# A hybrid decoder step on one core: a second bank for the third products, the last pair's second products one projection later, and the norms of x in two parts

## The chip, the cores and the metric

The kernel runs on one core of one Trainium2 chip. The metric is the device time of one execution in microseconds (us). A core has five engines with a queue each: TensorE (PE; its weight loads are shown apart, as PEld), VectorE (DVE), ScalarE (ACT), GpSimd (POOL) and SyncE (SP, which here only issues DMAs). Each engine works its queue in the order in which it was written, and engines wait for each other by semaphores. TensorE writes its results to PSUM, which has eight banks of 128 x 512 float32; all other tiles lie in SBUF, 128 partitions of one address space.

## The reference

One step of a one-layer decoder for 512 prompt tokens and 8 sequences of 8 new tokens (64 sample tokens) with 2048 cached tokens each. What matters here is the way into the layer and one of its three attention forms, the one over compressed blocks of the cache:

```python
def pre_mixer(x, c, lp):
    mod = jnp.einsum('bd,de->be', jax.nn.silu(c), lp['w_ada']) + lp['b_ada']
    sh1, sc1, gt1, sh2, sc2, gt2 = jnp.split(mod[:, None, :], 6, axis=-1)
    h = rms_norm(x, lp['norm1_g']) * (1.0 + sc1) + sh1
    z = jnp.einsum('btd,dc->btc', h, lp['w_in'])
    ...

def compress_blocks(x, pos, w1, w2):
    ...
    lead = jnp.einsum('bncgd,cdh->bngh', xc + pos[0], w1[0])
    trail = jnp.einsum('bncgd,cdh->bngh', xc + pos[1], w1[1])
    return jnp.einsum('bngh,hd->bngd', jax.nn.silu(lead[:, :-1] + trail[:, 1:]), w2)
```

`compress_blocks` is computed for the raw keys and the raw values (kv = 0 and 1 below) of all cached pages of the 8 sequences; the keys are then RMS-normed. Everything else (attention, the output projection, an MLP) comes later in the kernel and is not touched.

## The kernel before, in words

**The first stage** (`first_stage`, from L549) does two things at once. It compresses the cache of the 8 sequences, and it brings x into its normed, turned and modulated form `hf`.

The cache work is cut into 48 units. Sequences go in four pairs; the sequences of the first two pairs are taken one by one (units 0 to 31, eight for each sequence), those of the last two pairs two at a time (units 32 to 39 and 40 to 47). A unit is one of four quarters j of the taps, for keys or values. The DVE first copies a quarter of the pages into another order (`cmp_order`, tile `ro`, for keys and values together). PE transposes it (`rows_turn`, PSUM tiles `ct`), ACT copies the result to the tile `x`, and DVE or POOL adds its two halves to `xs`. Then come the products of the unit (`cmp_hidden`, L487): the first and second products `hid`, from `x`, into two PSUM banks per pair (one for keys, one for values), and the third products `hids`, from the sums `xs` and the summed weights `w1sum`, into one bank per pair that holds keys and values side by side. When the last quarter of a pair is done, `cmp_act` (L503) reads the banks `hid` (ACT, then DVE), `cmp_silu` (L522) subtracts from the bank `hids` (DVE writes `csx`), and takes the silu (tanh on ACT, a product on DVE, tile `cst`). Some units later `cmp_out` (L532) multiplies that with the second weights (`co`, the second products; ACT squares and a chain of small DVE operations norm the keys, `rms_cols`, L426), and `cmp_keys` (L542) turns the normed keys (`kct`).

The work on x is put in between by a table written by hand, `todo[u]`: lists of functions that run behind unit u. For each of the five tiles of x (four of 128 prompt tokens, one of 64 sample tokens) there is a load on the POOL queue (`load_x`, three buffers), `norm(k)` (`norm_scaled`, L742: ACT squares with a sum, a chain of 12 small DVE operations for the inverse root, `rsqrt`, L139, then ACT multiplies x by the root in place) and three units later `turned(k)` (eight PE transposes `nt` into two PSUM tiles, which ACT copies to `hf`). Eight chunks of the modulation weights are handled likewise: `ada_first` sums a chunk (PE into a PSUM tile `ada`, copied by ACT), and one unit later `ada_end` turns it (PE into a PSUM tile `adat`, read by a DVE reduction `adas`).

PSUM in the first stage (`banks`, L66, called at L2572 with 3): two banks `tr` for `ct`, three banks `mm` that serve `nt`, `ada`, `adat`, `co`, `kct` and a few more, two banks `acc` for `hid`, one bank `cc` for `hids`.

**The order of the work.** While `self.chain` is a string, `link` (L93) ties every PE instruction behind the one before it, so in the first stage and in the first projection PE does exactly the order of the program. The other engines' queues are ordered by the framework's scheduler, by a simulated time; `issue_after` holds an instruction behind another one of the same engine.

**The seam and the projections.** At unit 46 `seam` (L2547) frees the first stage's pool `pe`, splits the eight rows of `hf` into high and low parts (`split_pack`, L825, whose operation on DVE has L829, tiles `h2`) and splits the first two chunks of `w_in` (`winh` on ACT, `winl` on DVE). Behind unit 47 comes the silu of the last pair (`cmp_act` and `cmp_silu` for i = 3, whose tiles lie inside the tile `w1raw`, the first weights, and so appear under that name). Then eight projections follow, `step(0)` to `step(7)` (`project`, L883): each multiplies the five tiles of h with one chunk of 256 or 264 columns of `w_in`, 24 matrix products per prompt tile, 16 for the sample tile. `between` is a list of functions that run behind the products of tile 0, 1, ... In `step(0)` they are: nothing, `cmp_out` for the keys of the last pair, `cmp_out` for its values, `cmp_keys` and `room` (which takes the memory of `w1raw` for the next stage).

**Memory.** SBUF tiles lie in pools that are stacked from the left (`const`, `keep`, `small`, `op`, `pl`, `pe`, and later `op2`, `zn`, `pkq`, `pk`, `pm`, `pq`, `pu`, `pf`, ...) and from the right (`zf`, `pw`, `pc`, `ph`, ...). Every tile takes a multiple of 32 bytes per partition. In `keep` there are two tiles of two float32 each, `cmpb` and `cmpb2`. In the built program the pools on the left behind `keep` (`small`, `op` and those above) start at 32 modulo 64 bytes; the pools on the right start at 0 modulo 64.

Of the kernel before, what the change touches and what calls it, by code (L numbers as in the profile page):

```python
# [6 lines left out]
F32 = mybir.dt.float32  # L7
F32R = mybir.dt.float32r
BF16 = mybir.dt.bfloat16
I32 = mybir.dt.int32  # L10
AF = mybir.ActivationFunctionType
OP = mybir.AluOpType
AX = mybir.AxisListType

P = 128
D = 1024
# [3 lines left out]
NS = 64  # L20
# [3 lines left out]
TOK = 2080  # L24
# [10 lines left out]
TILES = [(0, 128), (128, 128), (256, 128), (384, 128), (512, 64)]  # L35
# [11 lines left out]
class Step:  # L47
# [347 lines left out]
    def cmp_bias(self, pe, kv):  # L395

        if kv == 0:
            self.cmpb = self.keep.tile([P, 2], F32, name="cmpb")
            self.posp = pe.tile([P, 256], F32, tag="posp", bufs=1, name="posp")
        pb = self.mmb(f"posb{kv}")  # L400
        for j in range(4):
            for i in range(4):
                n = 16 * kv + 4 * j + i
                self.mm(pb[32 * i:32 * i + 32, 0:P], self.posT[:, n:n + 1].to_broadcast([P, 32]),
                        self.w1raw[:, kv, 4 * j + i, :], j == 0, j == 3)
        (self.act if kv else self.cp)(self.posp[:, P * kv:P * kv + P], pb[:, 0:P])

    def cmp_bias_end(self):
        tb = self.sideb("posbt")
        for kv in range(2):  # L410
            self.tr(tb[:, P * kv:P * kv + P], self.posp[:, P * kv:P * kv + P])
        self.nc.vector.tensor_reduce(self.cmpb, tb[:, 0:256].rearrange("p (k i r) -> p k r i", k=2, i=4)[:, :, 0, :],
                                     axis=AX.X, op=OP.add)
        self.cmpb2 = self.keep.tile([P, 2], F32, name="cmpb2")
        self.ts(self.cmpb2, self.cmpb, 2.0, None, OP.mult)

    def silu2(self, pool, hb, W, bias, tag, uid, room=None):

# [68 lines left out]
    def cmp_hidden(self, u):  # L487
        i, bs, j, kv = self.units[u]
        first = bs[0] % 2 == 0 and j == 0
        if first and kv == 0:  # L490
            self.hid[i] = [self.accb(f"hid{i}{e}") for e in range(2)] + [self.bank("cc", 1, f"hids{i}")]
        ab, c = self.hid[i][kv], self.hid[i][2]
        x, xs = self.ring[u % 2]
        q, n = P * (bs[0] % 2), P * len(bs)
        for e in range(2):
            for a in range(2):
                self.mm(ab[:, 256 * e + q:256 * e + q + n], self.w1raw[:, kv, 8 - 8 * e + 4 * a + j], x[:, 2 * e + a, q:q + n],
                        first and e + a == 0, j == 3 and a == 1)
        for a in range(2):
            self.mm(c[:, 256 * kv + q:256 * kv + q + n], self.w1sum[:, kv, j, a], xs[:, a, q:q + n],  # L500
                    first and kv + a == 0, j == 3 and a == 1)

    def cmp_act(self, pl, i, kv):  # L503
        if kv == 0:
            self.ths, self.xbs = [], []

        v = self.r1.rearrange("p (n c) -> p n c", c=512)
        xb, th = (v[:, 1 if kv else 8], v[:, 0 if kv else 9]) if i == 3 else (
            pl.tile([P, 512], F32, tag="csx", bufs=2, name=f"csx{i}{kv}"), pl.tile([P, 512], F32, tag="cst", bufs=2, name=f"cst{i}{kv}"))
        ab = self.hid[i][kv]  # L510
        t, y = th[:, 0:256], th[:, 256:512]
        self.act(y, ab[:, 256:512], AF.Identity, bias=self.cmpb[:, kv:kv + 1])
        o = xb.rearrange("p (s c m e) -> p s m e c", s=8, c=8, e=2)
        av, yv = [a.rearrange("p (s m c) -> p s m c", s=8, m=4) for a in (ab[:, 0:256], y)]
        self.tt(o[:, :, 0:3, 1], yv[:, :, 0:3], av[:, :, 1:4], OP.add)
        self.tt(o[:, :, 3, 1, 0:7], yv[:, :, 3, 0:7], av[:, :, 0, 1:8], OP.add)
        self.tt(o[:, :, 3, 1, 7], yv[:, :, 3, 7], ab[:, 32:288].rearrange("p (s c) -> p s c", c=32)[:, :, 0], OP.add)
        self.stt(t, y, self.cmpb2[:, kv:kv + 1], ab[:, 0:256], OP.subtract, OP.add)
        self.ths.append(th)
        self.xbs.append(xb)  # L520
# [11 lines left out]
    def cmp_out(self, pl, i, kv):  # L532
        ob = self.mmb(f"co{i}{kv}")
        for s in range(4):
            self.mm(ob[:, 64 * s:64 * s + 64], self.ths[kv][:, P * s:P * s + P], self.w2[kv], True, True)
        if kv == 0:
            r = self.r1[:, 1024:1536].rearrange("p (n g d) -> p n g d", n=2, d=64) if i == 3 else None
            self.kn = self.rms_cols(pl, ob, P, 4, "kn", f"{i}", None if r is None else (r[:, 0], r[:, 1]))
        else:
            self.cp(self.vc[:, 2 * i:2 * i + 2, :], ob[:, 0:256].rearrange("p (b e) -> p b e", b=2))  # L540
# [8 lines left out]
    def first_stage(self, pl, pe, hf, seam):  # L549
# [3 lines left out]
        self.chain = ""  # L553
        self.sideb = self.mmb
        self.cpg, self.ros, self.hid, self.adas = {}, {}, {}, {}
        xs = []

        def load_x():
            k = len(xs)
# [2 lines left out]

        def norm(k):
            with self.tc.issue_after(self.last_high):
                self.norm_scaled(xs[k], 0, k, xs[k], pl.tile([P, D], BF16, tag="sq", name=f"sq{k}"))

        def turned(k):
            t0, m = TILES[k]
            for h in range(2):
                self.act(hf[:, 4 * h:4 * h + 4, t0:t0 + m], self.norm_turned(xs[k], 0, k, h))  # L570
# [37 lines left out]
        todo = {u: [] for u in range(48)}  # L608
# [3 lines left out]
        todo[10] += [self.ada_turned, lambda: self.cmp_bias(pe, 0), lambda: self.cmp_bias(pe, 1)]  # L612
        todo[12] += [self.cmp_bias_end]

        for k, u in enumerate((23, 25, 27, 29, 33)):
            todo[u - 3] += [lambda k=k: norm(k)]
            todo[u] += [lambda k=k: turned(k)]
        pages = lambda b: lambda: (self.cmp_tile(pe, b), self.cmp_pages("sync", b))
        wada = lambda k: lambda: self.ada_first_load(pe, ada[k])
# [119 lines left out]
        for a in range(3):  # L739
            self.tt(self.Dt[:, :, 4 * a, :], xv, pv[:, :, a + 1], OP.add)  # L740

    def norm_scaled(self, sq, n, i, x, junk=None):  # L742

        t0, m = TILES[i]
        ss = self.small.tile([P, 1], F32, tag="nss", name=f"nss{n}_{i}")
        self.squares = self.act((sq if junk is None else junk)[:m], x[:m], AF.Square, accum_out=ss[:m]).ins
        rs = self.small.tile([P, 1], F32, tag="nrs", name=f"nrs{n}_{i}")
        self.rsqrt(rs[:m], ss[:m], 1.0 / D)
        if n:
            self.ts(sq[:m], x[:m], rs[:m], None, OP.mult)  # L750
        else:
            self.act(sq[:m], x[:m], scale=rs[:m])

    def norm_turned(self, sq, n, i, h):

# [1769 lines left out]
    def run(self):  # L2525
        nc, I, O, keep = self.nc, self.I, self.O, self.keep
# [16 lines left out]
        lctx, actx, zctx, pctx = [ExitStack() for _ in range(4)]  # L2543
        pl, pe = self.pool("pl", lctx), self.pool("pe", actx)
        h2 = []

        def seam():  # L2547

            actx.close()
            self.zfp = self.pool("zf", zctx, side="right")  # L2550
            self.zF = self.zfp.tile([P, 4, C_N], F32, tag="zF", bufs=1, name="zF")
            self.pw, self.pc, ph = [self.pool(n, pctx, side="right") for n in ("pw", "pc", "ph")]
            last = self.splits[-1], self.last_high

            def rows(pins, ks):
                with ExitStack() as c:
                    for i in pins:
                        c.enter_context(self.tc.issue_after(i))
                    for k in ks:
                        h2.append(ph.tile([P, 2 * NT], F32R, name=f"h2_{k}"))  # L2560
                        self.split_pack(h2[k], hf[:, k])
                        self.splits.append(self.packed)

            self.wraw = {}
            self.win_load(self.pw, 0)
            rows(self.behind46, range(3))
            for i in range(2):
                self.win_split(self.pw, 0, i, last)
                rows(last, ((3, 4), (5, 6, 7))[i])

        with ExitStack() as c:
            self.banks("psc", c, 3)  # L2572
            self.first_stage(pl, pe, hf, seam)
        self.banks("ps", self.top, 4)
        lctx.close()
# [6 lines left out]

        self.znp = self.pool("zn", octx)
        self.zN = self.znp.tile([P, 4, TOK - C_N], F32, tag="zN", name="zN")

        def room():
            self.r1 = keep.tile([P, 5 * D], F32, tag="r1", bufs=1, name="r1w")
            self.zS = self.r1[:NS, 0:TOK]

        self.pkq = self.pool("pkq", octx)  # L2590
        kctx = ExitStack()
        pk = self.pool("pk", kctx)
        with pctx:
            pw, pc = self.pw, self.pc
            self.adn, self.ada_open, self.ada_next, self.ada_made = 8, None, None, None

            def step(ci, **kw):
                self.dma("sync", self.hfd[:, ci], h2[ci].bitcast(F32))
                self.project(pw, ci, h2, **kw)
                self.ada_later()  # L2600
                self.stage()

            step(0, between=[lambda: None] + [lambda kv=kv: self.cmp_out(None, 3, kv) for kv in range(2)] + [lambda: (self.cmp_keys(3), room())])
            self.chain = None
            self.cmp_prompt_a(pk, pc)
            self.cmp_prompt_load(pk, 0)
            step(1)
            self.cmp_prompt_b(0)
            self.cmp_prompt_load(pk, 1)
            self.head_norm("sk", C_SK, 2, 1)  # L2610
# [53 lines left out]
        ph = self.pool("p3", self.top, side="right")  # L2664
# [60 lines left out]
```

## Time and profile before

| | |
|---|---|
| Median of 3 runs | 1165.17 us (1164.33 to 1167.17) |
| The profiled execution's own time | 1162.46 us |
| Its span, first to last instruction | 1160.8 us, mean granted clock of TensorE 0.998 |
| First stage, about | 0 to 163 us |
| First projection, about | 163 to 185 us |
| Busy of 30 us, PE / DVE / ACT, from 90 us | 27.80 / 18.10 / 15.50 us |
| the same, from 120 us | 30.00 / 15.51 / 13.15 us |
| the same, from 150 us | 27.02 / 21.26 / 16.94 us |

How to read what follows: a row of the list of waits names the waiting engine, its instruction and what it waited for, then the total in us, how many times, and the longest. A row of the timeline has the start in us from the beginning of the span, the length, the engine, the line of the kernel, the operation, the tile written <- the tiles read, the shapes, the count of instructions merged, and in brackets the idle time ahead of it with what ended it. The end of a matrix product is modelled, so rows of PE overlap a little; the starts are measured. A row of the chain of work that ended last has start, length and what ran. In a table by windows a row has the window, its length, then for PE, PEld, DVE, ACT and POOL the busy time in it and the number of instructions, then the granted clock of TensorE, the mean share of the DMA engines and the GB/s.

### The profile page before, as it was taken

The page shows a single profiled execution, that of the slowest core. Times are in us where ns is not written, and L with a number is a line of the kernel's source. Part 1 is how long each engine was busy: PE and PEld are TensorE (multiplying, and loading weights), DVE is VectorE, ACT ScalarE, POOL GpSimd, SP SyncE. Part 2 cuts the span into 40 slices and gives each one's busy share as a digit, 9 for nine tenths or more (in the row PEclk, how much of TensorE's full clock was granted, in tenths as well). Part 3 has the DMA queues.
Part 4 walks back from the last instruction along what each step waited for, and adds up shares of the span by engine and source line. Part 5 has one row for each costly group of instructions (what it writes and reads, how often), then busy time and mean ns, then how long its engine had stood idle before and what let it go on. Part 6 is the DMA issues. An engine that isn't in the chain of part 4 may idle for free.

```text
span 1160.8 us, 25274 instructions
## 1 busy us (share of the span) xinstructions
PE 1128.4 (97%) x9530; PEld 970.0 (84%) x9530; DVE 763.8 (66%) x1852; ACT 578.4 (50%) x1101; POOL 301.7 (26%) x353
## 2 busy tenths in 40 slices
PE   8889989999999999999999999999999999999998
PEld 6887889999766566777899999789999997888887
DVE  3556474687786895666653545667766754897686
ACT  2365463354776785555532324356565654565420
POOL 4314320000220120001677662001655511101000
PEclk9999999999999999999999999999999999999999
DMA  9997444796684679899889986356454637877732
GB/s 236 248 269 231 127 141 166 240 336 215 196 274 147 207 225 306 292 318 322 228 255 299 335 267 218 101 153 214 133 155 148 193 115 251 318 260 245 223 116 82
DMA packets 188187, 255.51 MB, mean 220 GB/s; under 512 B 23161, under 2 KB 144706, under 8 KB 185890
## 3 DMA queue, kind: packets, MB, share of 16 engines
q1 hardware_dynamic: 148770, 173.03, 48.4%
q0 software_dynamic: 21296, 67.38, 18.0%
q10 hardware_dynamic: 18000, 13.50, 3.9%
q8 instruction: 75, 1.23, 0.4%
q14 instruction: 46, 0.38, 0.1%
HBM read 217.64 MB, written 57.12 MB: 237 GB/s over the span
## 4 chain that ended last, share of the span: by engine, by line
PE 81%; DVE 8%; DMA 6%; SPq 3%; issue 2%; ACT 1%; DVEq 0%; ACTq 0%
PE dn L83 14%; PE z L83 9%; PE mg L83 9%; DMA cpg<-in_cache_nsa_kv 5%; PE br L83 4%; PE wo L83 4%; PE up L83 3%; PE k L89 3%; SPq L168 2%; PE so L83 2%; PE hid L83 2%; PE ss L83 2%; PE dns L83 2%; PE ada L83 2%; PE ct L89 1%
## 5 line engine op out<-in xcount | busy, mean ns | idle before, releaser
L83 PE MATMUL z<-winh,h 128*128 128x264 f32 (+1 forms) x576 | 111.8, 288 | 0.1
L83 PEld LDWEIGHTS z<-winh,h 128*128 128x128 f32 x576 | 92.6, 192 | 1.6 <-issue 0.6
L83 PE MATMUL z<-winl,h 128*128 128x264 f32 (+1 forms) x320 | 88.6, 285 | 0.0
L83 PE MATMUL mg<-hH,wmh 128*128 128x288 f32 x240 | 70.2, 294 | 0.0
L83 PE MATMUL mg<-hH,wml 128*128 128x288 f32 x240 | 70.1, 294 | 0.0
L83 PE MATMUL mg<-hL,wmh 128*128 128x288 f32 x240 | 68.0, 293 | 0.0
L83 PE MATMUL hid<-x,w1raw 128*128 128x128 f32 (+1 forms) x384 | 64.4, 311 | 2.1 <-ACT x L118 2.1
L83 PEld LDWEIGHTS z<-winl,h 128*128 128x128 f32 x320 | 61.2, 191 | 0.1
L83 PEld LDWEIGHTS hid<-x,w1raw 128*128 128x128 f32 x384 | 54.2, 191 | 5.2 <-ACT x L118 2.6
L118 ACT ACTIVATE x<-ct 128x512 f32<-128x512 f32 x64 | 36.4, 594 | 41.9 <-PE ct L89 25.6
L137 DVE TENSOR_TENSOR wml<-wmr,wmh 128x1024 fp32r<-128x1024 f32 x14 | 19.7, 1405 | 43.2 <-ACT wmh L118 43.2
L83 PEld LDWEIGHTS mg<-hH,wmh 128*128 128x128 f32 x240 | 45.1, 188 | 0.1
L83 PEld LDWEIGHTS mg<-hH,wml 128*128 128x128 f32 x240 | 45.0, 187 | 0.0
L83 PEld LDWEIGHTS mg<-hL,wmh 128*128 128x128 f32 x240 | 44.3, 188 | 0.0
L137 DVE TENSOR_TENSOR wp<-sums,wp 128x1024 fp32r<-128x1024 f32 x26 | 36.6, 1415 | 9.7 <-ACT wp L118 9.2
L137 DVE TENSOR_TENSOR wp<-pu,wp 128x512 fp32r<-128x512 f32 (+1 forms) x26 | 30.4, 1176 | 19.1 <-ACT wp L118 15.6
L2083 POOL TENSOR_TENSOR td<-td 128x512 f32<-128x512 f32 x24 | 35.5, 1482 | 18.8 <-DMA td<-in_w_down 18.7
L83 PE MATMUL hids<-xs,w1sum 128*128 128x128 f32 (+1 forms) x192 | 36.1, 310 | 4.2 <-DVE csx L106 4.2
L118 ACT ACTIVATE u<-u 128x1152 f32<-128x1152 f32 x29 | 33.6, 1160 | 11.0 <-DVE u L106 10.3
L2083 POOL TENSOR_TENSOR td<-td,td 128x512 f32<-128x512 f32 x24 | 34.2, 1426 | 16.7 <-DMA td<-in_w_down 16.0
L89 PE MATMUL ct<-identF,ro 128*128 128x128 f32 x256 | 36.1, 275 | 2.3 <-DVE ro L121 2.3
L83 PE MATMUL br<-oH,wbl 128*128 128x288 f32 x128 | 37.8, 295 | 0.0
(1175 smaller groups left out, 3561.8 us busy)
## 6 DMA issues: line engine op xcount, KB each, us to landing
adw<-in_w_ada SPq DMA_DIRECT2D x16, 1024.0 KB
foxD<-in_cache_fox_kv SPq DMA_DIRECT2D x128, 128.0 KB
rows<-in_cache_nsa_kv SPq DMA_DIRECT2D x128, 128.0 KB
rows<-foxD SPq DMA_DIRECT2D x26, 512.0 KB
pu<-in_w_up SPq DMA_DIRECT2D x26, 512.0 KB
wdr<-in_w_down SPq DMA_DIRECT2D x26, 512.0 KB
cpg<-in_cache_nsa_kv SPq DMA_DIRECT2D x96, 128.0 KB
td<-in_w_down POOLq DMA_DIRECT2D x24, 512.0 KB, 6.4
```

Of the source, the lines that this page charges most:

```text
L83: ins = self.nc.tensor.matmul(out, a, b, start=start, stop=stop, skip_group_check=True)
L89: ins = self.nc.tensor.transpose(out, in_, self.identF[:n, :n])
L118: return self.nc.scalar.activation(out, in_, f, **kw)
L137: self.splits.append((eng or self.nc.vector).tensor_tensor(l, x, h.bitcast(F32), op=OP.subtract).ins)
L168: self.issued[eng] = getattr(self.nc, eng).dma_start(out, in_).ins
L2083: self.nc.gpsimd.tensor_tensor(out, x, y, op=OP.subtract)
```

## The change

- `hids` gets two banks (`cc` 1 to 2), taken in turn by the pairs; the shared banks `mm` of the first stage go from three to two, so that it stays at eight.
- `norm(k)` is cut in two: the squares and the inverse root (`norm_root`), and the multiplication of x by it on ACT (`scaled(k)`). They run behind units (18, 20, 22, 28, 29) and (21, 23, 25, 30, 31); before, both ran behind units (20, 22, 24, 26, 30). `turned(k)` stays at 23, 25, 27 and 33, except for the fourth tile, which goes from 29 to 32.
- The second products of the last pair (`cmp_out(3, .)`) and `cmp_keys(3)` move from the first projection into the second: behind its tiles 0, 1 and 3.
- The tile `last_ths` (4 KB per partition, in a pool `pt` of its own on the right) takes the silu of the last pair and the norm of its keys; they no longer lie inside `w1raw`. The tile `r1w` is taken ahead of the first projection.
- `cmpb2` becomes the second half of `cmpb`, so `keep` is 32 bytes shorter, and `small`, `op` and all pools above them on the left move down by 32 bytes, from 32 to 0 modulo 64. The pools on the right stay.

```diff
-            self.cmpb = self.keep.tile([P, 2], F32, name="cmpb")
+            self.cmpb = self.keep.tile([P, 4], F32, name="cmpb")
...
-        self.cmpb2 = self.keep.tile([P, 2], F32, name="cmpb2")
+        self.cmpb2 = self.cmpb[:, 2:4]
...
-            self.hid[i] = [self.accb(f"hid{i}{e}") for e in range(2)] + [self.bank("cc", 1, f"hids{i}")]
+            self.hid[i] = [self.accb(f"hid{i}{e}") for e in range(2)] + [self.bank("cc", 2, f"hids{i}")]
...
-        xb, th = (v[:, 1 if kv else 8], v[:, 0 if kv else 9]) if i == 3 else (
+        xb, th = (v[:, 8 + kv], self.last_ths[:, kv]) if i == 3 else (
...
-            r = self.r1[:, 1024:1536].rearrange("p (n g d) -> p n g d", n=2, d=64) if i == 3 else None
+            r = self.last_ths[:, 0].rearrange("p (n g d) -> p n g d", n=2, d=64) if i == 3 else None
...
         def norm(k):
             with self.tc.issue_after(self.last_high):
-                self.norm_scaled(xs[k], 0, k, xs[k], pl.tile([P, D], BF16, tag="sq", name=f"sq{k}"))
+                roots[k] = self.norm_root(xs[k], 0, k, xs[k], pl.tile([P, D], BF16, tag="sq", name=f"sq{k}"))
+
+        def scaled(k):
+            m = TILES[k][1]
+            self.act(xs[k][:m], xs[k][:m], scale=roots[k])
...
-        for k, u in enumerate((23, 25, 27, 29, 33)):
-            todo[u - 3] += [lambda k=k: norm(k)]
+        for k, (n, v, u) in enumerate(((18, 21, 23), (20, 23, 25), (22, 25, 27), (28, 30, 32), (29, 31, 33))):
+            todo[n] += [lambda k=k: norm(k)]
+            todo[v] += [lambda k=k: scaled(k)]
             todo[u] += [lambda k=k: turned(k)]
...
-            self.pw, self.pc, ph = [self.pool(n, pctx, side="right") for n in ("pw", "pc", "ph")]
+            self.pw, self.pc, ph, pt = [self.pool(n, pctx, side="right") for n in ("pw", "pc", "ph", "pt")]
+            self.last_ths = pt.tile([P, 2, 512], F32, name="cst3")
...
-            self.banks("psc", c, 3)
+            self.banks("psc", c, 2)
...
-            step(0, between=[lambda: None] + [lambda kv=kv: self.cmp_out(None, 3, kv) for kv in range(2)] + [lambda: (self.cmp_keys(3), room())])
+            step(0)
...
-            step(1)
+            step(1, between=[lambda kv=kv: self.cmp_out(None, 3, kv) for kv in range(2)] + [lambda: None, lambda: self.cmp_keys(3)])
```

More of the change, by code (lines that the diff above doesn't have):

```diff
@@ L411, in cmp_bias_end @@
             self.tr(tb[:, P * kv:P * kv + P], self.posp[:, P * kv:P * kv + P])
-        self.nc.vector.tensor_reduce(self.cmpb, tb[:, 0:256].rearrange("p (k i r) -> p k r i", k=2, i=4)[:, :, 0, :],
+        self.nc.vector.tensor_reduce(self.cmpb[:, 0:2], tb[:, 0:256].rearrange("p (k i r) -> p k r i", k=2, i=4)[:, :, 0, :],
                                      axis=AX.X, op=OP.add)
-        self.cmpb2 = self.keep.tile([P, 2], F32, name="cmpb2")
-        self.ts(self.cmpb2, self.cmpb, 2.0, None, OP.mult)
+        self.cmpb2 = self.cmpb[:, 2:4]
+        self.ts(self.cmpb2, self.cmpb[:, 0:2], 2.0, None, OP.mult)
     def silu2(self, pool, hb, W, bias, tag, uid, room=None):
@@ L555, in first_stage @@
         self.cpg, self.ros, self.hid, self.adas = {}, {}, {}, {}
-        xs = []
+        xs, roots = [], {}
         def load_x():
@@ L740, in forget_sums, with norm_root @@
             self.tt(self.Dt[:, :, 4 * a, :], xv, pv[:, :, a + 1], OP.add)
-    def norm_scaled(self, sq, n, i, x, junk=None):
+    def norm_root(self, sq, n, i, x, junk=None):
         t0, m = TILES[i]
@@ L748, in norm_scaled @@
         self.rsqrt(rs[:m], ss[:m], 1.0 / D)
[L749 to L752, printed above, removed]
+        return rs[:m]
+    def norm_scaled(self, sq, n, i, x, junk=None):
+        m = TILES[i][1]
+        self.ts(sq[:m], x[:m], self.norm_root(sq, n, i, x, junk), None, OP.mult)
     def norm_turned(self, sq, n, i, h):
@@ L2584, in run @@
         self.zN = self.znp.tile([P, 4, TOK - C_N], F32, tag="zN", name="zN")
-        def room():
-            self.r1 = keep.tile([P, 5 * D], F32, tag="r1", bufs=1, name="r1w")
-            self.zS = self.r1[:NS, 0:TOK]
+        self.r1 = keep.tile([P, 5 * D], F32, tag="r1", bufs=1, name="r1w")
+        self.zS = self.r1[:NS, 0:TOK]
         self.pkq = self.pool("pkq", octx)
```

## The prediction

> **What bounds the kernel now.** I read the page first: busy time, then the chain that ended last by engine.
>
> ```profile
> span 1160.8 us, 25274 instructions
> PE 1128.4 (97%) x9530; PEld 970.0 (84%) x9530; DVE 763.8 (66%) x1852; ACT 578.4 (50%) x1101; POOL 301.7 (26%) x353
> PE 81%; DVE 8%; DMA 6%; SPq 3%; issue 2%; ACT 1%; DVEq 0%; ACTq 0%
> ```
>
> PE is the bound: it works 97% of the span and carries 81% of the chain. The change adds and removes no matrix product, so it can only gain where PE stands still, and lose where PE is made to stand. Hence the second view, the waits of PE up to 215 us (first stage and two projections), and with it one row of the waits of DVE, which tells whether the page loads (`cpg`) set the pace.
>
> ```profile
> PE hids L83 <- DVE csx L106: 4.2, 2, 2.2
> PE co L83 <- DVE w1raw L115: 2.9, 1, 2.9
> PE hid L83 <- ACT x L118: 2.1, 2, 1.9
> PE nt L89 <- ACT x L118: 1.5, 1, 1.5
> DVE ro L121 <- DMA cpg<-in_cache_nsa_kv: 3.0, 3, 2.4
> ```
>
> The first four rows are the stops the change addresses: 4.2 + 2.9 + 2.1 + 1.5 = 10.7 us. The last says that the copies `ro` hardly wait for pages (3.0 us in 30 to 168 us), so a PE that runs ahead some us still finds its data. Because PE is nearly always busy behind 185 us, I let what is gained before it pass to the end in full.
>
> The profiled execution took 1162.46 us, 2.71 less than the median of 1165.17. I make the sum against 1162.46 and then take it from the median.
>
> **The second bank for `hids`.** The timeline shows both stops:
>
> ```profile
> 53.79 0.68 PE L83 MATMUL hids<-xs,w1sum 128*128 128x128 f32 x4 [1.98 <-DVE csx L106]
> 51.52 0.46 DVE L115 SCALAR_TENSOR_TENSOR cst<-cst,cmpb,hid 128x256 f32<-128x256 f32 x1
> 98.41 1.10 PE L83 MATMUL hids<-xs,w1sum 128*128 128x256 f32 x4 [2.19 <-DVE csx L106]
> 95.29 0.47 DVE L115 SCALAR_TENSOR_TENSOR cst<-cst,cmpb,hid 128x256 f32<-128x256 f32 x1
> ```
>
> The first products of the next pair must not write the one bank before `csx` has read it. With two banks that wait goes. What is late next? The `hid` banks stay at two, and their last reads are the rows `cst`, done at 51.52 + 0.46 = 51.98 and 95.76. PE's next product would begin at 53.79 - 1.98 = 51.81 and 98.41 - 2.19 = 96.22, with the `hid` of the values later still, so nothing replaces the wait. The second stop is worth its 2.2 us; the first I put together with the next part.
>
> **The norms in two parts.** ACT works in order, so an x that waits for its inverse root holds the copies of `ct` behind it:
>
> ```profile
> 69.10 1.15 ACT L118 ACTIVATE x<-x,nrs 128x1024 f32<-128x1024 f32 x1 [0.98 <-DVE nrs L115]
> 72.80 1.15 ACT L118 ACTIVATE x<-x,nrs 128x1024 f32<-128x1024 f32 x1 [2.55 <-DVE nrs L115]
> 70.30 1.09 PE L89 MATMUL nt<-identF,x 128*128 128x128 f32 x8 [1.48 <-ACT x L118]
> 75.46 1.16 PE L83 MATMUL hid<-x,w1raw 128*128 128x128 f32 x8 [1.85 <-ACT x L118]
> 73.00 0.60 PE L89 MATMUL ct<-identF,ro 128*128 128x128 f32 x4
> 71.51 0.15 DVE L112 TENSOR_SCALAR lfrow<-ptT 128x1 int32<-128x1 int32 x1 [2.38 <-DMA ptT<-in_page_table]
> 72.62 0.69 DVE L121 COPY ro<-cpg 128x1024 f32<-128x1024 f32 x1
> 50.78 1.93 POOL L168 DMA_DIRECT2D x<-in_x_prompt  x3
> ```
>
> The chain is: ACT waited 2.55 us for `nrs`, because DVE stood 2.38 us at `lfrow` for a DMA, in the midst of the root. In the changed kernel the roots begin two units earlier and the multiplication comes three units behind them, so ACT no longer waits there. Stops that this can free: 1.98 (first `hids`) + 1.48 + 1.85 = 5.3 us. But `lfrow` stays, and its DMA doesn't come earlier because PE does. What DVE has behind it, the `ro` copy for a later turn, ends no earlier than 71.51 + 0.15 + 0.69 = 72.35; with four turns (0.44 us between starts) the products at 75.46 could start at 72.8 at best. If the wait thus moves from ACT to PE by way of `ro`, 75.46 - 72.8 = 2.7 us remain of 5.3. Ends 2.7 and 5.3; I take 3.5, nearer the low one, since the DMA row is there to be read. The tiles of x are loaded at 50.78, and `norm(0)` now runs behind unit 18, near 58 us; I count nothing for it. No DMA is moved. The work per norm is the same.
>
> **The second products of the last pair.** Now they stand in the first projection, and PE, in written order, stops for them:
>
> ```profile
> 169.54 0.28 PE L83 MATMUL z<-winl,h 128*128 128x264 f32 x1
> 169.41 1.25 DVE L137 TENSOR_TENSOR winl<-winr,winh 128x1056 fp32r<-128x1056 f32 x1
> 172.69 1.51 PE co L83 x8
> 174.20 4.12 PE z L83 x24
> 178.32 0.84 PE co L83 x8
> 179.16 2.96 PE z L83 x24
> 182.12 0.22 PE kct L89 x2
> 185.79 12.97 PE z L83 x107
> 174.20:176.50 2.30, 2.30 (x11) 2.30 (x12) 1.61 (x9) 0.38 (x1) 0.00 (x0) 0.50 0.92 261
> 178.40:184.30 5.90, 5.90 (x51) 5.90 (x51) 1.40 (x6) 0.91 (x3) 0.00 (x0) 1.00 1.09 391
> ```
>
> Two costs lie here. The stop itself is 2.9 us: PE is through with its first tile at about 169.8 and starts `co` at 172.69. And behind it the granted clock is 0.50 in the first row of the windows (third number from the end), 1.00 again in the second. The same work shows the price in the chain: `co` 1.51 against 0.84, 24 products `z` 4.12 against 2.96, together 0.67 + 1.16 = 1.8 us. In the second projection `co` stands over 16 us later, so its silu is long done; `co` for the keys to `kct` took 182.12 - 172.69 = 9.4 us here, and there three tiles of `z` (24 x 0.121 = 2.9 us each, from 12.97 / 107) and 0.84 lie between, 9.5 us: no new wait, or a few tenths. The next tile of `z` needs only halves of `w_in`, the last of which is done at 169.41 + 1.25 = 170.66; that may keep up to 0.8 of the 2.9, and I count that to the range. Moved `co`, root and `kct` cost the same there; their DVE work goes behind the splits of the next chunk. Gain 2.9 + 1.8 = 4.7 us, ends 2.9 and 4.7.
>
> The Trainium skill's page "TensorE: Matmul & The Clock Gate", section "What's actually happening", has the half clock come after at least one idle window of about 3.4 us. Here the trace differs: the clock fell after a stop of 2.87 us. By the page, the stop alone would not have lowered it, taking the stop away would not give the clock back, and the sum would be 1.8 us smaller.
>
> **Two shared banks where there were three.** This is the price. I went through the 35 uses of these banks in written order (10 `nt`, 8 `ada`, 8 `adat`, 6 `co`, 3 `kct`). Where a use of the third bank had its reader done, nothing changes. At units 35 and 43 the order is `ada`, `co` of the keys, `adat`, `co` of the values: with two banks the last one must wait until the keys' bank has been read, by `knn`.
>
> ```profile
> 114.16 1.00 PE L83 MATMUL co<-w2rawv,cst 128*128 128x64 f32 x8
> 115.12 0.41 DVE L106 TENSOR_TENSOR knn<-co,knr 128x256 f32<-128x256 f32 x1
> 149.32 1.00 PE L83 MATMUL co<-w2rawv,cst 128*128 128x64 f32 x8
> 150.28 0.41 DVE L106 TENSOR_TENSOR knn<-co,knr 128x256 f32<-128x256 f32 x1
> L118 ACT ACTIVATE adw<-nt x6: 587/594/598, 77.5 to 88.3; 128x512 f32<-128x512 f32 x6
> ```
>
> 115.53 - 114.16 = 1.37 and 150.69 - 149.32 = 1.37 us, 2.7 in all. Behind the waiting `co` the whole PE queue waits, and `vc` and the copies `ro` behind it on DVE shift along. Three more places (units 27, 32, 33) have a third tile right behind two `nt`; ACT reads one `nt` in 0.594 us (here `hf` has the name `adw`), PE writes one in 0.44, so each waits some 0.3 us: 0.9. Together 3.6 us. Ends 0 (the waits fall into others) and 6 (the root's chain on DVE gets later with its work).
>
> **Places modulo 64 bytes.** In the stages that follow, the moved pools feed many products, and those behind them are the rows to compare:
>
> ```profile
> L83 PE MATMUL mg<-hH,wmh 128*128 128x288 f32 x240 | 70.2, 294 | 0.0
> L83 PE MATMUL br<-oH,wbl 128*128 128x288 f32 x128 | 37.8, 295 | 0.0
> ```
>
> The streamed operand lies in a moved pool in about 1260 products; two forms of one shape, one streamed from 0 and one from 32 modulo 64, last 294 and 295 ns. At 1 ns each that is 1.3 us to either side. I count nothing and keep 1.3 for the range. `last_ths`, `r1w` taken earlier and `cmpb2` inside `cmpb` add no instruction.
>
> **The sum.** 3.5 + 2.2 + 4.7 - 3.6 = 6.8 us gained: 1162.46 - 6.8 = 1155.7 for an execution like the profiled one, 1165.17 - 6.8 = **1158.4** on the median. What a measurement of this kernel can tell from no change is about 0.3%, 3.5 us.
>
> **Rivals.** *More is gained*: `lfrow` never reaches PE (5.3) and the bank waits vanish (0): 5.3 + 2.2 + 4.7 = 12.2 us, 1153.0. For it: DVE is only 66% busy; against: the two waits for `knn` can be read off.
> *The waits change places*: the stage's gains of 5.7 go into bank waits and `lfrow` (2.7 + 2.2 - 5 = 0), and the seam gives its 2.9 without the clock: 1162.3, within 0.3%. The change not doing what it says belongs here: if PE stopped at the `hid` banks instead of at `hids`, 4.2 would be gone from the sum, 1162.6. Against that stand the rows `cst`, ended before PE's turn.
> *The clock isn't given back* (by the mechanism that something other than the stop at 172.69 lowered it): 4.7 becomes 2.9, sum 5.0, 1160.2. For it: the stops of 1.98 and 2.19 us have no such price that I saw in the rows behind them; against: it began with the product behind the longest stop. The page of the Trainium skill cited above speaks for this one.
> *Slower*: two shared banks for 35 tiles in written order. If every tile waited for the reading of the bank before it, 0.594 us by the ACT row, that is 35 x 0.594 = 20.8 us against gains of 10.4: 10.4 slower, 1175.6. It decides from (10.4 + 3.5) / 35 = 0.4 us per tile on the mean. For it: ACT and DVE work in order, so a reading can stand behind other work; against: most of these tiles come singly, with products of a unit between, and my count is 0.1 us per tile.
>
> **How the numbers follow.** The forecast 0.52, more gained 0.18, changed places 0.14, clock 0.08, slower 0.08. Faster by over 0.3% (below 1161.7): 0.52 + 0.18 + 0.08 = 0.78; within: 0.14; slower: 0.08. The range goes from the larger gain with the 1.3 us of the places, 1165.17 - 12.2 - 1.3 = 1151.7, rounded to 1151, to the low ends together, 2.7 + 2.2 + 2.9 - 5 = 2.8 less 1.3 = 1.5, 1163.7, rounded to 1163.5; only the slower case and the edges lie outside.
>
> **What would show it.** In the profile after, no wait of `hids` for `csx`, none of `nt` or `hid` over 1 us for ACT's x near 70 us unless a `ro` copy behind `lfrow` stands there, no stop ahead of a `co` in the first projection, and a granted clock of 1.00 through it. New waits: `co` for `knn` at units 35 and 43, near 1.4 us each. The first projection ends some 6 to 7 us earlier than before, and the time from there to the end is the same within 1.3 us. Wrong would be: a clock of 0.5 elsewhere near the seam, bank waits over 6 us in sum, or a changed duration per product behind 215 us.

## The result and the profile after

The changed kernel takes 1152.47 us (median of 4 runs, 1151.95 to 1153.99) against 1166.17 us of the kernel before, timed beside it (1164.33 to 1171.01): a ratio of 0.9878, 95% interval 0.9846 to 0.9911. The interval lies clear of 1: the kernel is faster, by 1.2%. The time is inside the range on record (1151 to 1163.5), but 5.9 us below the value named there (1158.4): the gain is 13.7 us where 6.8 were forecast. The profiled execution takes 1152.51 us, 9.95 less than the profiled one of before.

The page of the changed kernel, busy times first:

```profile
span 1150.8 us, 25271 instructions
PE 1124.5 (98%) x9530; PEld 969.6 (84%) x9530; DVE 762.1 (66%) x1852; ACT 577.8 (50%) x1101; POOL 300.3 (26%) x353
```

PE issues the same 9530 products; its busy time falls by 3.9 us, its idle time by 6.1. The waits of PE in 0 to 215 us (engine, line, releaser: total us, times, longest):

```profile
PE idle L83 <- DVE identB L110: 2.3, 1, 2.3
PE co L83 <- DVE adas L322: 1.9, 2, 0.9
PE ada L83 <- ACT adw L118: 1.5, 1, 1.5
PE ct L89 <- DVE ro L121: 1.3, 2, 0.7
PE co L83 <- DVE r1w L106: 1.0, 1, 1.0
PE hids L83 <- DVE xs L483: 0.8, 1, 0.8
PE adat L89 <- ACT adw L118: 0.5, 2, 0.2
PE hid L83 <- ACT x L118: 0.2, 1, 0.2
```

Of the four addressed stops (10.7 us) only 0.2 us under an old name is left. Five new rows stand in their place, 1.9 + 1.5 + 1.0 + 0.8 + 0.5 = 5.7 us. Here are all but the last of them in the timeline of the changed kernel; under three of them stand the DVE rows that bear on the wait (two under the first):

```profile
110.38 1.10 PE L83 MATMUL co<-w2rawv,cst 128*128 128x64 f32 x8 [0.94 <-DVE adas L322]
110.10 0.23 DVE L322 TENSOR_REDUCE adas<-adat 128x18 f32<-128x72 f32 x1
110.24 0.41 DVE L106 TENSOR_TENSOR knn<-co,knr 128x256 f32<-128x256 f32 x1
146.73 1.10 PE L83 MATMUL co<-w2rawv,cst 128*128 128x64 f32 x8 [0.93 <-DVE adas L322]
94.26 1.07 PE L83 MATMUL ada<-wada,adw 128*32 128x256 f32 x16 [1.47 <-ACT adw L118]
71.69 0.71 PE L83 MATMUL hids<-xs,w1sum 128*128 128x128 f32 x4 [0.79 <-DVE xs L483]
70.63 0.21 DVE L112 TENSOR_SCALAR lfrow<-ptT 128x1 int32<-128x1 int32 x2 [1.98 <-DMA ptT<-in_page_table]
183.64 0.55 PE L83 MATMUL co<-w2rawv,cst 128*128 128x64 f32 x3 [0.96 <-DVE r1w L106]
183.17 0.42 DVE L106 TENSOR_TENSOR r1w<-z,r1w 64x264 f32<-64x264 f32 x1
```

The first `co` starts 0.05 us behind the end of `adas` (110.10 + 0.23 = 110.33), while `knn` still runs until 110.65: it waits for the bank of `adat`, and in the built program that is the one it gets. The bank of the keys isn't the one waited for.

Put side by side product by product, the two timelines differ by these amounts (start in the changed kernel less start before): -2.6 us at the end of the first stage (`co` at 146.73 against 149.32), -5.6 behind the first two projections (`ada` at 193.12 against 198.70), -10.0 at the end. So 2.6 came from the first stage, 3.0 from the seam, and 4.4 from stages that the diff doesn't touch. The medians gain another 3.75 us that the two profiled executions don't show.

The 4.4 us are in the groups by form behind 215 us. First the kernel before, then the changed one (count | busy us, mean ns of one):

```profile
L83 PE MATMUL dn<-wdT_0h,as 128*128 128x512 f32 x64 | 20.0, 395 | 0.0
L83 PE MATMUL wo<-wo0h,mix 128*128 128x512 f32 x36 | 11.8, 400 | 0.0
L83 PE MATMUL dn<-wd61l,u 128*128 128x512 f32 x20 | 7.9, 396 | 0.0
L83 PE MATMUL mg<-hL,wmh 128*128 128x288 f32 x240 | 68.0, 293 | 0.0
```

```profile
L83 PE MATMUL dn<-wdT_0h,as 128*128 128x512 f32 x64 | 19.6, 389 | 0.0
L83 PE MATMUL wo<-wo0h,mix 128*128 128x512 f32 x36 | 11.7, 396 | 0.0
L83 PE MATMUL dn<-wd61l,u 128*128 128x512 f32 x20 | 7.9, 395 | 0.0
L83 PE MATMUL mg<-hL,wmh 128*128 128x288 f32 x240 | 68.6, 296 | 0.0
```

The 512-column products with `as` and `mix` as stationary operand are 4 to 6 ns shorter in their rows, those with `u` in the row shown are not, and the 288-column ones in the row shown are slightly longer. From start to start, the mean of `dn` with `as` goes from 233.3 to 226.8 ns (600 products), of `wo` from 233.2 to 228.0 (211): 3.9 + 1.1 = 5.0 us. The products `mg` give 1.2 us back; the rest of the difference is in waits, which vary by themselves: a second profile of the changed kernel (below) needs 951.2 us from that `ada` to its last product, this one 953.6 and the one of before 958.1.

### The profile page after: what moved, and what is told of

It reads as the page before. It is cut to its first block, busy times and chain, and to the rows that moved or that the text cites. A ratio compares the mean times of both kernels' runs of the same rounds, so it can differ in the third digit from the quotient of the medians.

```text
span 1150.8 us, 25271 instructions
## 1 busy us (share of the span) xinstructions
PE 1124.5 (98%) x9530; PEld 969.6 (84%) x9530; DVE 762.1 (66%) x1852; ACT 577.8 (50%) x1101; POOL 300.3 (26%) x353
## 5 line engine op out<-in xcount | busy, mean ns | idle before, releaser
L118 ACT ACTIVATE u<-u 128x1152 f32<-128x1152 f32 x29 | 33.6, 1160 | 11.5 <-DVE u L106 10.7
L83 PE MATMUL br<-oL,wbh 128*128 128x288 f32 x128 | 37.8, 295 | 0.0
L83 PE MATMUL br<-oH,wbh 128*128 128x288 f32 x128 | 37.7, 294 | 0.0
L89 PE MATMUL k<-identF,rows 128*128 128x128 f32 x256 | 35.7, 280 | 2.0 <-ACT kt L118 1.5
```

The source lines that it names most:

```text
L83: ins = self.nc.tensor.matmul(out, a, b, start=start, stop=stop, skip_group_check=True)
L89: ins = self.nc.tensor.transpose(out, in_, self.identF[:n, :n])
L118: return self.nc.scalar.activation(out, in_, f, **kw)
```

## The experiments

All runs were timed in five rounds beside the kernel before, whose median there was 1165.8 to 1167.2 us. Pitches are means over the products from start to start in the trace; places are the operands' addresses in the built program.

**Places.** Theory P: the place of the operands sets the pitch of the 512-column products. Rival R: the later stages gain because work starts earlier. The first run undoes the merging of `cmpb2` in the changed kernel, the second does only that in the kernel before:

```diff
-            self.cmpb = self.keep.tile([P, 4], F32, name="cmpb")
+            self.cmpb = self.keep.tile([P, 2], F32, name="cmpb")
...
-        self.cmpb2 = self.cmpb[:, 2:4]
+        self.cmpb2 = self.keep.tile([P, 2], F32, name="cmpb2")
```

> The changed kernel, but with cmpb2 as a tile of its own again, so that the pools on the left return to 32 modulo 64. Theory P (the place of the stationary operand against the streamed one sets the pitch of the 512-column products): dn and wo go back from 227 to 233 ns from start to start, which over some 830 products is 5 us, the 288-column products win back about 1 us, and the time is 1156 to 1157 against 1152.5. Rival R (what was gained behind the second projection comes from work that starts earlier): the pitch stays at 227 and the time at 1152 to 1153.

Measured: 1155.4 us (ratio 0.9892, 0.9866 to 0.9919), pitch of `dn` 233.3 ns again.

> The kernel before with cmpb2 as the second half of cmpb and nothing else. Theory P: dn and wo at 227 ns, 4 to 5 us faster than the kernel before (ratio 0.996). Rival R: the ratio is 1.000 and the pitch 233.

Measured: 1161.87 us, ratio 0.9959 (0.9940 to 0.9978), 5 us by itself, and pitch 227.0 ns. P holds for the pitch in both directions, and for the time in the second run; the first by its time alone can't be told from the changed kernel. R falls: in the second run's profile what follows the second projection starts later than before (`ada` at 202.46 against 198.70), and the pitch is 227 all the same.

What place? The next two runs keep all on the left at 0 modulo 64:

```diff
-            self.cmpb = self.keep.tile([P, 4], F32, name="cmpb")
+            self.cmpb = self.keep.tile([P, 20], F32, name="cmpb")
```

and, in the second of them, also

```diff
-        self.pool("edge", self.top, side="right").tile([P, 8], F32, name="edger")
+        self.pool("edge", self.top, side="right").tile([P, 24], F32, name="edger")
```

> The changed kernel with 64 bytes more in keep: the pools on the left stay at 0 modulo 64, but the stationary operand of dn and wo goes from 64 to 0 modulo 128, while the streamed one stays at 64. If what counts is the place modulo 64, the pitch stays at 227 ns and the time at 1152.5. If what counts is that both operands have the same place modulo 128, the pitch is 233 and the time 1156 to 1157.

> As the one before, and the pools on the right shifted by 64 bytes too, so that both operands of dn and wo lie at 0 modulo 128. If the same place modulo 128 counts: 227 ns, 1152 to 1153. If the place of the stationary operand at 64 counts by itself: 233 ns, 1156 to 1157. If only the place modulo 64 counts: 227 ns here and in the one before.

Measured: 1154.14 us and 233.3 ns; 1154.86 us and 232.7 ns. The place modulo 64 doesn't decide (first), nor does the same place modulo 128 (second). The second leaves "the stationary operand at 64 by itself", but `dns` of that run contradicts it: streamed from 128 and stationary at 128 modulo 256, it takes 227.9. Sorted by the difference of the two places modulo 256, all six profiles agree: 227 to 229 at 0 (231 to 232 in eight products `dns` with `as`), 232 to 233 at 128, 192 and 224. The changed kernel has both in one profile: of its `dn` with `u`, 109 at a difference of 192 take 233.3, and 99 at 0 take 227.0. (The times moved less than the pitch let expect; medians of six runs that spread over 4 to 7 us don't settle 4 us. The profiles do: from `ada` behind the projections to the last product, the four with 232 ns or more need 955.9 to 958.1 us, the ten with 227, later runs included, 951.1 to 953.9.) So the theory became Q: what counts is that difference. It says that an edge of 56 floats on the right in place of 24 must be fast, also for `u`:

> The changed kernel with 64 bytes more in keep on the left and 192 on the right, so that streamed and stationary operand of dn, dns and wo all have the same place modulo 256 (0 and 0). Theory Q (the pitch of a 512-column product depends on the difference of the two places modulo 256, read from all six profiles so far): 227 ns for all of them, also for the 112 products dn whose stationary operand is u and that now take 233; 0.5 to 1 us faster than the changed kernel. Rivals (the place of the stationary operand at 64 modulo 128 counts, or of the streamed one): 233 ns, 4 to 5 us slower than the changed kernel.

Measured: 1149.67 us (1148.23 to 1150.44), ratio 0.9859 (0.9824 to 0.9893); 226.9 ns for `dn` with `as` and with `u`. By its median it is 2.8 us faster than the changed kernel, where 0.5 to 1 was expected; the intervals of the two ratios overlap. The group of `u` shows it too:

```profile
L83 PE MATMUL dn<-wd61l,u 128*128 128x512 f32 x20 | 7.8, 390 | 0.0
```

| run | streamed, stationary of `dn` with `as`, modulo 256 | difference | ns from start to start |
|---|---|---|---|
| before | 192, 224 | 224 | 233.3 |
| changed | 192, 192 | 0 | 226.8 |
| left + 64 | 192, 0 | 192 | 233.3 |
| left + 64, right + 64 | 128, 0 | 128 | 232.7 |
| left + 64, right + 192 | 0, 0 | 0 | 226.9 |

Why the difference counts wasn't tried and stays open.

**Parts undone.** The theory on the clock arose from the profile of the places alone, that is, of the kernel before as to order. Its windows show the granted clock (third number from the end), beside the stops:

```profile
53.07 0.68 PE L83 MATMUL hids<-xs,w1sum 128*128 128x128 f32 x4 [1.98 <-DVE csx L106]
53.90:57.80 3.90, 3.90 (x23) 3.90 (x22) 0.90 (x2) 0.70 (x2) 1.11 (x2) 0.56 1.02 322
77.54 1.62 PE L83 MATMUL hid<-x,w1raw 128*128 128x128 f32 x7 [3.03 <-ACT x L118]
77.90:81.90 4.00, 4.00 (x24) 4.00 (x23) 2.09 (x14) 1.89 (x5) 0.00 (x0) 0.58 0.94 203
176.43 1.64 PE L83 MATMUL co<-w2rawk,w1raw 128*128 128x64 f32 x8 [2.86 <-DVE w1raw L115]
176.90:180.90 4.00, 4.00 (x22) 4.00 (x22) 2.46 (x14) 0.38 (x1) 0.00 (x0) 0.58 0.86 235
```

Three of the stops that the change addresses are each followed, within a microsecond, by some 3.4 us of half clock. In the profile of before on record only the last was. By the trace's record of the clock, the half clocks begin at 53.95, 77.84 and 176.83 us and last 3.41 us each. The distances, 23.89 and 98.99 us, are 7 and 29 times 3.413 us, so the clock falls only at points of a fixed step, whose place differs from one execution to the next. The stop of 1.98 us at `hids` thus cost the clock in this execution and not in the one of before. What decides at such a point isn't found: of the 3.41 us up to 53.75, such a point in the profile of before (35 steps ahead of 173.22), PE was idle for 1.94 us, and the clock stayed at 1.00.

The norms put back:

```diff
-        for k, (n, v, u) in enumerate(((18, 21, 23), (20, 23, 25), (22, 25, 27), (28, 30, 32), (29, 31, 33))):
-            todo[n] += [lambda k=k: norm(k)]
-            todo[v] += [lambda k=k: scaled(k)]
+        for k, u in enumerate((23, 25, 27, 29, 33)):
+            todo[u - 3] += [lambda k=k: norm(k)]
+            todo[u - 3] += [lambda k=k: scaled(k)]
```

> The changed kernel with norm, scaling and turning behind the units of the kernel before (20, 22, 24, 26, 30 and 23, 25, 27, 29, 33). Theory (ACT held by the root stops PE, and in executions that the phase of the clock's window decides, the half clock follows): stops of nt and hid for ACT's x near 67 to 72 us come back, 2.4 us in the profile (3.3 less the 0.8 that PE waits there for xs now), mean granted clock of the timed runs below that of the changed kernel by 0.001 to 0.003, in all 3 to 5 us slower than 1152.5, ratio to the kernel before 0.991. Rival (lfrow sets the pace there anyway, the waits only changed names): less than 1 us slower, clock unchanged.

Measured: 1154.32 us (1151.93 to 1159.7), ratio 0.9907 (0.9873 to 0.9940). The stops came back:

```profile
PE hid L83 <- ACT x L118: 2.5, 2, 2.3
PE nt L89 <- ACT x L118: 1.5, 1, 1.5
```

PE was 3.8 us behind the changed kernel at 73.5 us, but 2.4 of it returned at `ada` (there, at unit 32, the fourth tile is turned late in the changed kernel), and at 184 us the two were 0.2 apart. In the profile the rival is right, by another way than it said: the new places of the norms bring 3.8 and pay them back. The median is 0.9 to 1.9 us above the two of the changed kernel (1153.4 and 1152.47), less than the 3 to 5 expected and within the spread.

One bank for `hids`, three shared ones (`cc` 2 to 1, `banks` 2 to 3):

> The changed kernel with one bank for hids and three shared ones. Theory: the two stops of hids for csx return (2 us each), the stops of co for the two shared banks (1.1 each) and of ada (1.5) go; in the profile 0 to 1 us slower, and by the granted clock (two stops of 2 us, which can bring the half clock for 3.4 us, price 1.7 each when they do) 1 to 4 us slower in the timed runs. Rival (two shared banks cost as much as the second bank brings, the clock has nothing to do with it): 1152.5 within 1, clock unchanged.

Measured: 1155.38 us (1152.87 to 1157.28), ratio 0.9904 (0.9869 to 0.9940), clock 0.997 to 0.999 in the six runs. Its profile has the stops and, 1.1 us behind the first of these (55.9), a half clock:

```profile
PE hids L83 <- DVE csx L106: 4.1, 2, 2.1
57.00:60.80 3.80, 3.80 (x22) 3.80 (x21) 0.64 (x2) 0.98 (x2) 1.11 (x2) 0.55 1.01 313
```

At 184 us it is 3.7 us behind, 3.3 of them the price of two half clocks: read from the steps between the two timelines, 1.6 and 1.7. The other one stood at 33.15 to 36.57, 7 steps of 3.413 us earlier, behind a stop of 1.75 us for a late page, and has nothing to do with the banks. What the exchange of banks wins by waits alone is within half a microsecond of nothing, as expected; what it is worth in this profile is the one half clock behind `hids`. By the timed runs alone this version can't be told from the changed kernel.

The last pair back in the first projection:

```diff
-            step(0)
+            step(0, between=[lambda: None] + [lambda kv=kv: self.cmp_out(None, 3, kv) for kv in range(2)] + [lambda: self.cmp_keys(3)])
...
-            step(1, between=[lambda kv=kv: self.cmp_out(None, 3, kv) for kv in range(2)] + [lambda: None, lambda: self.cmp_keys(3)])
+            step(1)
```

> The changed kernel with the second products of the last pair back in the first projection, behind its tiles 1, 2 and 3. Theory: PE stops about 3 us for the silu, the half clock follows for 3.4 us, and the time is 3 to 5 us over 1152.5 with a mean clock lower by 0.001 to 0.002. Rival (the stop only moved to the second projection, where the second bank wait of 1.0 us stands): under 2 us.

Measured: 1155.99 us (1153.3 to 1157.52), ratio 0.9906 (0.9871 to 0.9941), clock 0.997 to 0.999; in the profile 4.7 us behind at the end of the second projection.

```profile
PE co L83 <- DVE cst L115: 2.9, 1, 2.9
170.30:177.10 6.80, 6.77 (x31) 6.77 (x32) 3.35 (x17) 0.43 (x2) 0.00 (x0) 0.51 0.91 283
```

The same stop of 2.9 us is followed by 6.8 us of half clock here, two steps of 3.41, and by one before: the price of a stop isn't fixed.

**Again, and better.** The changed kernel on one chip with two successors:

> The changed kernel itself, on one chip with the two that follow: 1152 to 1154, mean granted clock 0.999 to 1.000 in nearly all runs, against 0.991 to 0.997 for the kernel before. If the clock theory holds, the kernel before is slower the lower its mean clock, by about 1.2 us for each 0.001.

Measured: 1153.4 us (1149.68 to 1155.84), ratio 0.9891 (0.9858 to 0.9924), clock 0.998 to 1.000. The clock theory can be read from the kernel before, which ran 50 times beside these experiments, with mean clocks of 0.990 to 0.997:

| mean granted clock | runs | median us |
|---|---|---|
| 0.990 to 0.992 | 14 | 1169.8 |
| 0.993 to 0.995 | 19 | 1167.1 |
| 0.996 to 0.997 | 17 | 1163.4 |

A line through the 50 falls 1.2 us for each 0.001 (correlation -0.83) and gives 1162.1 at 0.998, the clock of the profiled execution, which took 1162.46. The half clocks themselves ask for that slope: one of 3.41 us costs 1.7 us and takes 1.7 / 1161 = 0.0015 off the mean, which is 1.16 us for each 0.001. Not all is clock: the changed kernel at 0.999 took 1150.4 and 1155.4. What else varies is open.

> The changed kernel with the second products of the values one unit later for the second and third pair (units 36 and 44) and the fourth tile of x turned behind unit 31 instead of 32. Theory (PE waits at the two shared banks because two uses follow each other too closely): the two stops of co (0.9 each by the waits, 1.1 by the starts) and that of ada (1.5) go, at most 0.3 comes back at adat; 2.5 to 3.5 us faster than the changed kernel in the profile. Rival (the silu or the readers are late anyway, PE waits elsewhere for the same): within 1 us of it.

```diff
-        for k, (n, v, u) in enumerate(((18, 21, 23), (20, 23, 25), (22, 25, 27), (28, 30, 32), (29, 31, 33))):
+        for k, (n, v, u) in enumerate(((18, 21, 23), (20, 23, 25), (22, 25, 27), (28, 30, 31), (29, 31, 33))):
...
-                todo[(18, 34, 42)[i] + kv] += [lambda i=i, kv=kv: self.cmp_out(pl, i, kv)]
+                todo[(18, 34, 42)[i] + kv * (2 if i else 1)] += [lambda i=i, kv=kv: self.cmp_out(pl, i, kv)]
```

Measured: 1152.22 us (1149.16 to 1157.45), 1.2 below the changed kernel beside it, span 0.5 below it; at the `ada` behind the projections it is 1.4 us ahead (191.24 against 192.66). That is less than the 2.5 to 3.5 expected and as the rival had it. The stops of `co` for `adas` went, but that of `ada` only changed its name, and grew:

```profile
PE adat L89 <- ACT adw L118: 2.6, 3, 2.1
```

At unit 31 `adat` follows the two `nt` and waits for the copy of the first.

> The one before, with the places of the run that had 64 bytes more on the left and 192 on the right: the two gains add up to some 5 us, 1147 against 1152.5, ratio to the kernel before 0.983.

Measured: 1151.1 us (1148.07 to 1159.4), not 1147. In its profile the new stop brought the half clock:

```profile
94.46 0.44 PE L89 MATMUL adat<-identF,adap 128*128 128x128 f32 x2 [2.09 <-ACT adw L118]
```

with the granted clock at 0.50 from 94.94 to 98.35 us, mean 0.997, span 1152.4. It isn't the only half clock of this profile: another stands at 33.50 to 36.91, exactly 18 steps of 3.413 us earlier, behind a stop of `ct` of 1.43 us for a late page. A stop well under 2 us can thus be followed by it too. The last run spaces the uses out, with the fourth tile at (26, 28, 29):

> The changed kernel with the places of the run with 64 bytes on the left and 192 on the right, the second products of the values one unit later (36, 44), and the fourth tile of x normed, scaled and turned behind units 26, 28 and 29. Theory (what counts is that no use of the two shared banks follows two others closely): no stop of co, and none of ada or adat over 0.5 us between 80 and 105 us, so no stop over 2 us that could bring the half clock there; 2 to 3.5 us under the run with the places alone (1149.67), near 1147, mean clock 0.999 to 1.000. Rival (x of the fourth tile or its root comes too late at 29, PE waits at nt or hid instead): 1149 to 1152, with a stop of nt or hid for ACT's x.

Measured: 1148.16 us (1145.76 to 1153.62), ratio 0.9848 (0.9819 to 0.9878), span 1144.6; no stop of `co`, `ada` or `nt` is left, `adat` has 0.5. That is 1.5 us below the run with the places alone, where 2 to 3.5 were expected, and the ranges overlap; two of the six runs have a clock of 0.997 and 0.998 and take 1153.62 and 1152.87, so half clocks still occur. By its median this is the best version of the study, 4 to 5 us below the changed kernel.

## Why the prediction was right or wrong

**What bounds, and the first stage: right.** With every gain before 185 us passed on, the stage was to bring 3.5 + 2.2 - 3.6 = 2.1 and brought 2.6. The pieces are larger on both sides: the stops of `hids`, `nt` and `hid` gave 2.1 + 2.4 + 1.5 + 1.8 less 0.9 (PE waits behind `lfrow`, as foreseen, but by way of `xs` and not of `ro`) = 6.9 against 5.7, and 0.9 more fell away at a `ct` at 82.9 that I had not listed. The shared banks took 1.1 at each `co` (1.37 foreseen) and 2.3 + 0.4 + 0.3 elsewhere (0.9 foreseen): 5.2 against 3.6. The step mis-sized is "each waits some 0.3 us": at unit 32 ACT reads `nt` late, since it stands at a tanh of the silu. I had counted the length of a reading, not its place in ACT's queue:

```profile
93.09 0.63 ACT L118 ACTIVATE cst<-csx 128x512 f32<-128x512 f32 x1 [0.81 <-DVE csx L106]
93.63 1.06 ACT L118 ACTIVATE adw<-nt 128x512 f32<-128x512 f32 x2
```

The two waits of `co` came, but not for the reader that was named. "Must wait until the keys' bank has been read, by `knn`" holds when the two banks go strictly in turn; in the built program the second `co` gets the bank of `adat`, and waits for `adas`, which DVE does just ahead of `knn`, behind the root's chain. So the size was nearly right for a neighbouring reason.

**The seam: right mechanism, too large.** 4.7 forecast, 3.0 gained. The clock was 1.00 throughout, as foreseen. What I missed is a bank wait in the second projection (0.96 us at 183.64): `co` of the values needs the bank whose sum `r1w` stands behind `winl`, which waits for `winh` and so for its load. The other 0.7 us lie in small steps between the products and stay open. "No new wait, or a few tenths" was wrong; I had looked for a wait for data there, not for a bank.

**Places modulo 64: wrong.** "I count nothing and keep 1.3 for the range" should have been 4 to 5 us gained. The prediction's own sign of being wrong, "a changed duration per product behind 215 us", is there, and the time from the projections to the end is 4.4 us shorter, not the same within 1.3. I compared 288-column forms by the place of the streamed operand alone. Two things failed: the form (512 columns carry it) and the operand (the place of the stationary one relative to it). In the 288-column form `mg` with `wmh` even loses 1 to 2 ns per product; the other long groups move by 1 ns or less, either way. The rows of `dn` and `wo` stood in the profile, at 395 to 400 ns; `dns`, with both operands at the same place (227.9 ns from start to start), was there as the row to compare with.

**From the profiled execution to the median: wrong.** "I make the sum against 1162.46 and then take it from the median" assumes that the 2.71 us between them stay. They didn't: the profiled execution had lost clock at one stop only (mean 0.998), a typical run of the kernel before loses at several (median 0.994 in the 50 runs). With the stops gone, the changed kernel has 0.999 to 1.000 in the four runs of the result (0.998 to 1.000 in the six later ones). By the line above, 0.994 to 0.998 is worth some 4.8 us, which covers the 3.75 that the profiles don't show; the clocks of the four runs behind the median of before aren't on record, so this is an estimate. The stops of 2.0 us did have a price; in that one execution none was due. Where the prediction says that these stops "have no such price that I saw", that was true of one execution and taken for a rule.

The Trainium skill's page "TensorE: Matmul & The Clock Gate", section "What's actually happening", calls the window free-running, so that the same kernel varies with its phase: the runs agree, since the same stop was followed by a half clock in one profile and not in another, and the half clocks of one execution begin whole multiples of 3.413 us apart. It puts the idle time at one window of about 3.4 us; here stops of 1.43, 1.98, 2.1 and 2.9 us were enough, and the measurement decides.

So half of the gain came by the way forecast, and the other half by two terms that the sum put at nothing: 0.5 more in the first stage, 1.7 less at the seam, 4.4 from places and 3.75 from the clock come to 7.0 beyond 6.8. That the result lies inside the range is luck: its lower end, 1151, was made of larger gains in the first stage, which didn't come. (The upper end holds a slip: it takes 5 us for the banks, where the part on them ends at 6.) Of the rivals, "more is gained" comes nearest in time, but not for its reasons: the bank waits stayed.

## What to carry to other kernels

A stop of PE costs its length and, by chance of phase, some 1.7 us of half clock or twice that: read the granted clock of many runs, not of one profile, before subtracting. For long streams of products compare the two operands' places relative to each other (here modulo 256 bytes), form by form, before calling a shift of memory free. When a buffer is taken from a shared set, ask for each use where the reader of the last one stands in its engine's queue, not how long it takes.

## What was not expected of the hardware

Two 512-column products differ by 6.4 ns (226.9 against 233.3 from start to start, 3%) by where their operands lie: equal modulo 256 bytes is fast. In the 264-column products equal places are fastest too, but by less and in no clear order (means over the profiles): 119.3 ns at equal places, 119.9 at a difference of 96, up to 123.4 at 224. In the 288-column ones they aren't: 132.5 at equal places, 132.2 at 64, 133.5 at 128. And a stop of 1.4 to 2 us is enough for a half clock of 3.4 us, at some phases; one of 2.9 us was followed by 6.8 us. The half clocks of one execution begin whole multiples of 3.413 us apart.
